# An encoder layer on one core: where the halo tokens of the first half are normalised, and where the position bias is built

## The chip, the core and the metric

The kernel runs on one core of a Trainium2 chip. A core has TensorE (matmuls; PE in the profile, its weight loads PEld), VectorE (DVE), ScalarE (ACT), GpSimd (POOL) and SyncE (SP), which issues most of the transfers between the chip's main memory and the on-chip memory SBUF. Matmuls write to the accumulator memory PSUM, of eight banks here in two groups of four. Each engine works through its own queue in order and waits on semaphores for the others. The metric is device time in microseconds (us) of one execution.

## What is computed

One residual layer for 1024 tokens of width 1024, in float32. Its matmuls run in a reduced-precision form of float32 on operands that are split in a high and a low part, so that a product is three matmuls: high x high, high x low, low x high.

```python
h = rmsnorm(x, norm1_g) * (1.0 + sc1) + sh1        # sc1, sh1: silu(c) @ w_ada + b_ada
z = h @ w_in
u, v, q, k, va, gate_a, gate_b = jnp.split(z, cuts, axis=-1)
a_out = gmlp_branch(u, v, gm_v_g, gm_w_s, gm_b_s) @ w_a
b_out = window_attention_branch(q, k, va, q_norm_g, k_norm_g, attn_sink) @ w_b
merged = jax.nn.sigmoid(gate_a) * a_out + jax.nn.sigmoid(gate_b) * b_out
x = x + gt1 * (merged @ w_o)
h2 = rmsnorm(x, norm2_g) * (1.0 + sc2) + sh2
f_gate, f_up = jnp.split(h2 @ w_ffn_in, 2, axis=-1)
x = x + gt2 * ((jax.nn.silu(f_gate) * f_up) @ w_ffn_out)
```

`rmsnorm` divides each token by the root of the mean of its squares. The attention sees 128 tokens to either side; its logits get a bias of minus slope times distance, and tokens further than 128 are masked with a very large negative number. The slope of head h (from 0) is 2 to the power of -(h+1).

## The kernel before

x is kept transposed: the 1024 features lie in eight slices of 128 partitions, tokens along the columns. The tokens are done in two halves of 512 (`half(hf)`). Since the window reaches 128 tokens over the edge, the first half needs k and v of 128 tokens of the second one as well; these are the **halo** (`xh`, eight slices of 128x128 in the tile `halo`).

The start of the first half, up to line 742: SP loads x, the condition and the first weights. While these are on the way VectorE builds the bias of four heads (`bias_base`, `build_bias`): |key - query| in `d0`, the mask in `d1`, and for each head `d0 * -slope + d1` in bfloat16. Then come squares of x, their sums over the features by matmuls with ones into `total`, and the reciprocal roots in `rcol[0]`.

The first stage is the loop over eight slices `k` (line 749; the text calls one pass of it step k). For each, VectorE scales x by the column of `mod` and by the roots (`mid<-mid,mod,ss` in the profile), ScalarE adds the shift and rounds to the high part (`h<-mid,mod`, array `hH`), VectorE makes the low part (`hL`). The columns of `mod` for the next slice are made in `ada_dot`: VectorE multiplies a slice of the modulation weights with the condition and sums, ScalarE casts a weight if there is one to cast (`cast`), and then adds the bias into `mod`. TensorE multiplies the four token tiles with 512 columns of the q weight into four banks of PSUM (`qps`), a "q pass", and with 256 columns of the k and v weight (`kps`), a "k pass", three of each per step. From step 1 on a pass of high x high comes first; the k passes of step 4 are put off to step 5 (`late`).

A q weight serves two steps, a k weight (`w_kv`) four. They are loaded whole (`raw`), then ScalarE casts the high part (`wh`) and VectorE subtracts for the low part (`wl`); `wpool` has three buffers for each of the three. Casts stand at steps 1, 3 and 5 for the next q weight and at step 4 for the second k weight. A buffer is free when the last instruction that uses it is done.

The halo in the kernel before: `load` of `xh` on SP in step 1, squares by ScalarE in step 2 into `qh`, their sums by eight matmuls with ones in step 2 between passes (`tot4[:, 0:1]`; the profile shows each as two), root and reciprocal in step 3, spread over the partitions by a transpose on TensorE in step 3. `halo_four` scales four slices (VectorE), modulates them (four ScalarE instructions) and casts; `halo_low` makes the low parts; `halo_products` multiplies with the k weight, twelve matmuls for four slices. They run for slices 0 to 3 in step 4 and for slices 4 to 7 in step 7. The other four heads of the bias are built by VectorE in step 7.

Within the loop and behind it, `in_order[0]` is set: an engine's instructions keep the order in which the program gives them. An instruction that waits therefore holds all that follow on its engine.

Behind the loop: `wvs` takes the first weight of v (`unit`: load, ScalarE cast, VectorE low part; not bound to the order), ScalarE and VectorE copy q and k out of PSUM (`qraw`, `kraw`), `v_product(k)` multiplies slice k with the v weight, `kv_norms` and `q_norm` make norms (`kms` is the profile's name for the sums of squares of k), `turn_k` transposes k on TensorE. The second half, the attention, the gates and the feed-forward part follow; the change doesn't touch them.

Of the kernel before, what the change touches and what calls it, by code (L numbers as in the profile page):

```python
# [11 lines left out]
AF = mybir.ActivationFunctionType  # L12
# [14 lines left out]
NH = 8  # L27
# [10 lines left out]
ZEROS = (9, 1)  # L38
BIAS = 4

# [66 lines left out]
def kernel(  # L107
    ctx: ExitStack,
    tc: tile.TileContext,
    xA: bass.AP,  # L110
    xB: bass.AP,
    cols: bass.AP,
    rowv: bass.AP,
# [231 lines left out]
    def bias_base():  # L345
        d0, d1 = tmp()[:, :384], tmp()[:, :384]
        G.iota(d0, pattern=[[1, 384]], base=-P, channel_multiplier=-1,
               allow_small_or_imprecise_dtypes=True)
        V.tensor_scalar(d1, d0, -1.0, None, op0=ALU.mult)
        V.tensor_tensor(d0, d0, d1, op=ALU.max)  # L350
        V.tensor_scalar(d1, d0, float(P), NEG, op0=ALU.is_gt, op1=ALU.mult)
        return d0, d1

    def build_bias(d0, d1, heads):
        for h in heads:
            V.scalar_tensor_tensor(
                out=bias[:, h, :], in0=d0, scalar=-(2.0 ** -(h + 1)), in1=d1, op0=ALU.mult,
                op1=ALU.add,
            )

# [286 lines left out]
    def half(hf):  # L647
# [4 lines left out]
        if hf == 0:  # L652
# [3 lines left out]
            halo = midt(F32, 16)  # L656
            xh, qh = halo[:, :KT, :], halo[:, KT:, :]
            hl4 = midt(F32R, 16)
# [18 lines left out]
            A.activation(sm(QPK, "es"), ones[:, :QPK], AF.Silu)  # L677
            build_bias(*base_bias, range(BIAS))

# [69 lines left out]
        for k in range(KT):  # L749
            if hf == 0:  # L750
# [25 lines left out]
                if k == 0:  # L776
                    rb = ss_tile()[:, :HALF]
                    A.copy(rb, rp)
                    kbk.append(at_bank())
                    kps = [kbk[t // 2][:, (t % 2) * 256 : (t % 2 + 1) * 256] for t in range(nkv)]  # L780
                elif k == 2:
                    A.activation(qh, xh, AF.Square)
                elif k == 3:
                    A.activation(root[:, NT:], tot4[:, 0:1], AF.Sqrt, scale=1.0 / D, bias=epsc)

# [17 lines left out]
                fours = slice(0, 4), slice(4, 8)  # L803
                if k == KT // 2:
                    halo_four(fours[0])
                    wk_halo = wk
                elif k == KT - 1:
                    halo_four(fours[1])

# [4 lines left out]
                if k == 1:  # L814
                    load(wk0[:, 512:], wk_half[1])
                    load(xh.rearrange("p a b -> p (a b)"), xA[:, KT * HALF :])
                cast = (w_next[0], raw) if src is not None else None
                if k < KT - 1:
                    ada_dot(r[:, 0, :], SC1 + k + 1, cast, dot=None if k else dot1[:, :1])
                if k == 3:  # L820
                    V.reciprocal(rcol[0][:, NT:], root[:, NT:])
                V.scalar_tensor_tensor(out=hL[k // 4][:, k % 4, :], in0=x, scalar=sh,
# [6 lines left out]
                if k < KT - 1:  # L829
                    ada_dot(r[:, 1, :], SH1 + k + 1)  # L830
                if k == KT - 1:
                    build_bias(*base_bias, range(BIAS, NH))
                if k in (KT // 2, KT - 1):
                    halo_low(fours[k == KT - 1])
                if src is not None:
# [33 lines left out]
            for group in ((q_parts, k_parts) if hf == 1 and k == 4 else (q_parts + k_parts,)):  # L869
# [14 lines left out]
                for p, (e, part) in enumerate(passes):  # L884
                    if (hf, k, p) == (0, 2, 1):
                        for a in range(KT):
                            T.matmul(tot4[:, 0:1], qh[:, a, :], ones[:, 0:1], start=a == 0, stop=a == KT - 1)
                    elif (hf, k, p) == (0, 3, len(passes) - 1):
                        T.transpose(tot4[:, P : 2 * P], rcol[0][:, NT:].to_broadcast([P, P]), ident)
                    for ps, st, w, o, n, first, last in part:  # L890
                        for e1 in ((0, 1) if e is None else (e,)):
                            T.matmul(ps, st[e1 // 2], w[e1 % 2][:, o : o + n],
                                     start=k + e1 == 0 and first,
                                     stop=bool(k == KT - 1 and e1 == 2 and last))
            if hf == 0 and k == KT // 2:
                halo_products(fours[0], wk_halo)
            if hf == 0 and k == KT - 1:
                halo_products(fours[1], wk)
            if k % 2 == 1 and k < KT - 1:
# [15 lines left out]
        kraw, banks = [], []  # L915
        for b in range(3):
            w = 512 if hf == 0 and b < 2 else 256
            r = attp.tile([P, 512], F32, tag="pt", name=nm("kraw"), bufs=6)
            (V.tensor_copy if b % 2 else A.copy)(r[:, :w], kbk[b][:, :w])
            banks.append((r, w))  # L920
            kraw += [r[:, i : i + 256] for i in range(0, w, 256)]

# [75 lines left out]
        vps = [mm_bank() for _ in range(NT)]  # L998
        wvs.append(unit(w_v[1], V))
        kr = kv_norms(banks, nkv)  # L1000
        v_product(0)
        qr = [q_norm(qraw[:, t, :]) for t in range(2)]
# [1332 lines left out]
def _layout(inputs):  # L2335
# [30 lines left out]
    for w in (w_q, w_kv):  # L2366
# [3 lines left out]
                              for t in (slice(0, 512), slice(512, 640))], axis=1),  # L2370
        "xB": xt[:, 512:],
        "cols": np.concatenate([col(a["b_ada"][0]), col(a["norm1_g"][0]), col(a["norm2_g"][0]),
                                a["gm_b_s"][0].T, col(a["c"][0])], axis=1),
# [38 lines left out]
```

## Time and profile before

| | |
|---|---|
| three runs | 1212.48, 1213.0, 1214.31 us; median 1213.0 |
| the profiled execution | 1212.33 us, its span 1210.3 us |
| granted TensorE clock | 1.0 |
| moved from and to main memory | 241.00 MB, mean 199 GB/s |
| chain that ended last | TensorE 97%, VectorE 2% of the span |

The span is the time from the first to the last instruction of the profiled execution; 2.03 us lie around it. In the profile's lists `out<-in` names the tile that is written and those that are read, with buffer numbers left out: `mm` and `at` are the two groups of PSUM banks, `mid` a pool of eight large buffers in which x, the halo, the modulation weights and others lie. Most of the lines carry L143, the helper through which engines are called, so instructions are told apart by their tiles. Matmuls overlap in their ends; how long a row of them takes is read from the starts.

### The profile page before, as it was taken

The numbers are of one execution on the slowest core, as the hardware profiler recorded it, in microseconds if no ns is written. First come the engines' busy times: TensorE is split into PE (matmuls) and PEld (weight loads), VectorE is DVE, ScalarE is ACT, GpSimd is POOL, SyncE is SP. The second block draws the span as 40 slices with busy tenths as digits, with TensorE's granted clock in tenths as the row PEclk, the third lists the DMA queues.
The fourth block names the chain that finished last, engine by engine and source line by source line (L and its number), as shares of the span: only waits on it lengthen the run. The fifth ranks groups of instructions, "written<-read, shape, count | busy, mean of one in ns | idle before, by whom it ended". The sixth has DMA issues, their size and how long they took to land.

```text
span 1210.3 us, 15628 instructions
## 1 busy us (share of the span) xinstructions
PE 1204.0 (99%) x5640; PEld 1005.0 (83%) x5640; DVE 928.4 (77%) x1503; ACT 585.8 (48%) x958; POOL 156.6 (13%) x190
## 2 busy tenths in 40 slices
PE   9999999999999999999999999999999999999998
PEld 7888888888888888888888888888888888888887
DVE  9999977889978886898987757676676765765647
ACT  6667855367855533745553333333333334433341
POOL 0124323024322000002000000010000000000001
PEclk9999999999999999999999999999999999999999
DMA  9752168753177643567313545554555449995552
GB/s 373 283 188 91 36 227 314 294 218 130 71 265 273 210 145 102 170 228 270 105 61 109 187 178 206 191 192 158 195 198 197 157 164 374 393 355 191 191 174 105
DMA packets 79709, 241.00 MB, mean 199 GB/s; under 512 B 9104, under 2 KB 9360, under 8 KB 74384
## 3 DMA queue, kind: packets, MB, share of 16 engines
q1 hardware_dynamic: 64000, 165.55, 39.1%
q0 software_dynamic: 15632, 74.46, 16.3%
q8 instruction: 44, 0.72, 0.2%
q14 instruction: 33, 0.27, 0.1%
HBM read 178.63 MB, written 61.34 MB: 198 GB/s over the span
## 4 chain that ended last, share of the span: by engine, by line
PE 97%; DVE 2%; ACT 0%; DMA 0%; issue 0%; SPq 0%; DVEq 0%; ACTq 0%
PE mm L143 49%; PE at L143 48%; DVE mid L143 1%; DVE wl L143 0%; DMA mid<-in_xA_dram 0%; ACT mid L143 0%; DVE h L143 0%; ACT wh L143 0%; ACT h L143 0%; SPq L200 0%; DVE wh L143 0%; ACT mod L143 0%; ACT cc L143 0%; DVEq L143 0%; DVE rcol L143 0%
## 5 line engine op out<-in xcount | busy, mean ns | idle before, releaser
L143 ACT CAST wh<-raw 128x1024 fp32r<-128x1024 f32 (+1 forms) x154 | 157.3, 1023 | 110.8 <-PE mm L143 45.2
L143 DVE TENSOR_TENSOR wl<-raw,wh 128x1024 fp32r<-128x1024 f32 (+1 forms) x141 | 165.3, 1176 | 53.3 <-ACT wh L143 52.7
L143 PE MATMUL mm<-mid,wh 128*128 128x512 f32 x640 | 197.4, 390 | 0.0
L143 PEld LDWEIGHTS mm<-mid,wh 128*128 128x128 f32 x640 | 119.8, 188 | 24.7
L143 PE MATMUL mm<-wh,h 128*128 128x512 f32 x384 | 124.6, 396 | 0.4 <-ACT h L143 0.3
L143 PE MATMUL mm<-mid,wl 128*128 128x512 f32 x320 | 124.5, 389 | 0.0
L143 PE MATMUL mm<-h,wh 128*128 128x512 f32 x304 | 94.3, 391 | 0.0
L143 PE MATMUL at<-h,wh 128*128 128x512 f32 x304 | 93.8, 390 | 0.0
L143 PEld LDWEIGHTS mm<-wh,h 128*128 128x128 f32 x384 | 70.8, 188 | 14.1 <-ACT h L143 0.7
L143 DVE TENSOR_TENSOR wl<-ws,wh 128x1024 fp32r<-128x1024 f32 (+1 forms) x50 | 55.9, 1117 | 24.1 <-ACT wh L143 24.1
L143 PE MATMUL mm<-wl,h 128*128 128x512 f32 x192 | 71.2, 391 | 0.0
L143 PEld LDWEIGHTS mm<-mid,wl 128*128 128x128 f32 x320 | 60.1, 188 | 12.5
L143 PEld LDWEIGHTS at<-h,wh 128*128 128x128 f32 x304 | 56.9, 188 | 11.8
L143 ACT CAST wh<-ws 128x1024 fp32r<-128x1024 f32 (+1 forms) x50 | 48.4, 968 | 37.4 <-DVE ws L143 25.0
L143 PEld LDWEIGHTS mm<-h,wh 128*128 128x128 f32 x304 | 56.6, 188 | 11.6
L143 ACT ACTIVATE t<-t 128x512 f32<-128x512 f32 x46 | 28.5, 631 | 70.8 <-DVE t L143 70.8
L143 DVE TENSOR_TENSOR ol<-raw,oh 128x1024 fp32r<-128x1024 f32 x30 | 36.6, 1224 | 30.8 <-ACT oh L143 29.1
L143 PE MATMUL mm<-h,wl 128*128 128x512 f32 x152 | 59.2, 389 | 0.0
L143 PE MATMUL at<-h,wl 128*128 128x512 f32 x152 | 59.2, 389 | 0.0
L143 ACT ACTIVATE xs<-xs 128x512 f32<-128x512 f32 x21 | 13.3, 634 | 93.7 <-DVE xs L143 93.7
L143 ACT CAST oh<-raw 128x1024 fp32r<-128x1024 f32 x30 | 31.7, 1056 | 44.1 <-PE at L143 20.0
L143 PE MATMUL at<-wl,wh 128*128 128x512 f32 (+1 forms) x136 | 52.7, 388 | 0.0
(299 smaller groups left out, 2879.7 us busy)
## 6 DMA issues: line engine op xcount, KB each, us to landing
mid<-in_w_ada_dram SPq DMA_DIRECT2D x30, 512.0 KB, 7.9
raw<-in_w_gate_dram SPq DMA_DIRECT2D x26, 512.0 KB, 4.0
tA<-hid POOLq DMA_DIRECT2D x11, 1024.0 KB, 5.2
tB<-hid POOLq DMA_DIRECT2D x11, 1024.0 KB, 5.3
wo<-in_w_out_dram POOLq DMA_DIRECT2D x22, 512.0 KB, 6.1
wS<-wo POOLq DMA_DIRECT2D x11, 1024.0 KB, 5.4
raw<-wS SPq DMA_DIRECT2D x44, 256.0 KB, 3.2
raw<-tB SPq DMA_DIRECT2D x44, 256.0 KB, 5.3
```

The costliest lines, as they stand in the source:

```text
L143: ins = f(*args, **kw)
```

## The change

The input gets one more array, `xT`: the rows of x from token 512 on, one token per partition. The rest is in `half` and the two bias functions.

- Bias: the mask becomes part of the distance, which is 1e33 larger beyond 128; a head is then a multiplication by -slope. All eight heads are built at the start, two by ScalarE and six by VectorE.
- The halo's loads (128 token rows, and `xh`) are issued in step 6. Its mean squares are made in step 6 by ScalarE from the token rows, with a sum along each row, then root, reciprocal (VectorE) and the transpose on TensorE ahead of that step's last pass.
- The first four slices of the halo are scaled and cast in step 7 and multiplied behind step 7's passes; the other four are scaled in step 7, their low parts made behind the second v weight's, their products behind `v_product(0)`. The copy of the halo's k and v out of PSUM follows those.

```diff
-        V.tensor_scalar(d1, d0, float(P), NEG, op0=ALU.is_gt, op1=ALU.mult)
-        return d0, d1
-    def build_bias(d0, d1, heads):
-        for h in heads:
-            V.scalar_tensor_tensor(
-                out=bias[:, h, :], in0=d0, scalar=-(2.0 ** -(h + 1)), in1=d1, op0=ALU.mult,
-                op1=ALU.add,
-            )
+        V.tensor_scalar(d1, d0, float(P), FAR, op0=ALU.is_gt, op1=ALU.mult)
+        V.tensor_tensor(d0, d0, d1, op=ALU.add)
+        return d0
+    def build_bias(dist):
+        for h in range(NH):
+            slope = -(2.0 ** -(h + 1))
+            if h < BIAS:
+                A.mul(bias[:, h, :], dist, slope)
+            else:
+                V.tensor_scalar(bias[:, h, :], dist, slope, None, op0=ALU.mult)
...
-            build_bias(*base_bias, range(BIAS))
+            build_bias(base_bias)
...
-                elif k == 2:
-                    A.activation(qh, xh, AF.Square)
-                elif k == 3:
-                    A.activation(root[:, NT:], tot4[:, 0:1], AF.Sqrt, scale=1.0 / D, bias=epsc)
...
                 if k == KT // 2:
+                    wk_halo = wk
+                elif k == KT - 2:
+                    load(rows_h, xT[:P, :])
+                    load(xh.rearrange("p a b -> p (a b)"), xA[:, KT * HALF :])
+                elif k == KT - 1:
                     halo_four(fours[0])
-                    wk_halo = wk
-                elif k == KT - 1:
-                    halo_four(fours[1])
...
                 if k == 1:
                     load(wk0[:, 512:], wk_half[1])
-                    load(xh.rearrange("p a b -> p (a b)"), xA[:, KT * HALF :])
...
-                if k == 3:
-                    V.reciprocal(rcol[0][:, NT:], root[:, NT:])
...
-                if k == KT - 1:
-                    build_bias(*base_bias, range(BIAS, NH))
-                if k in (KT // 2, KT - 1):
-                    halo_low(fours[k == KT - 1])
+                if k == KT - 2:
+                    A.activation(rows_h, rows_h, AF.Square, accum_out=root[:, NT:])
+                    A.activation(root[:, NT:], root[:, NT:], AF.Sqrt, scale=1.0 / D, bias=epsc)
+                    V.reciprocal(rcol[0][:, NT:], root[:, NT:])
+                elif k == KT - 1:
+                    halo_low(fours[0])
+                    halo_four(fours[1])
...
-                    if (hf, k, p) == (0, 2, 1):
-                        for a in range(KT):
-                            T.matmul(tot4[:, 0:1], qh[:, a, :], ones[:, 0:1], start=a == 0, stop=a == KT - 1)
-                    elif (hf, k, p) == (0, 3, len(passes) - 1):
+                    if (hf, k, p) == (0, KT - 2, len(passes) - 1):
                         T.transpose(tot4[:, P : 2 * P], rcol[0][:, NT:].to_broadcast([P, P]), ident)
...
-            if hf == 0 and k == KT // 2:
+            if hf == 0 and k == KT - 1:
                 halo_products(fours[0], wk_halo)
-            if hf == 0 and k == KT - 1:
-                halo_products(fours[1], wk)
...
-        for b in range(3):
+        def copy_k(b):
...
+        for b in range(2 + hf):
+            copy_k(b)
...
         wvs.append(unit(w_v[1], V))
+        if hf == 0:
+            halo_low(fours[1])
+        v_product(0)
+        if hf == 0:
+            halo_products(fours[1], wk)
+            copy_k(2)
         kr = kv_norms(banks, nkv)
-        v_product(0)
```

## What was predicted, and from what

> **What bounds the kernel now.** I read the page's list of engines first, then busy time by stretches, then the first 80 us of the timeline.
>
> ```profile
> PE 1204.0 (99%) x5640; PEld 1005.0 (83%) x5640; DVE 928.4 (77%) x1503; ACT 585.8 (48%) x958; POOL 156.6 (13%) x190
> ```
>
> ```profile
> 15.00:25.00 10.00, 9.96 (x58) 8.69 (x58) 10.00 (x16) 6.60 (x12) 0.00 (x0) 1.00 1.03 411
> ...
> 75.00:1210.30 1135.30, 1131.65 (x5229) 942.89 (x5227) 859.22 (x1361) 540.17 (x865) 145.52 (x177) 1.00 0.54 193
> ```
>
> The columns of a stretch are length, busy PE, weight load, DVE, ACT, POOL, granted clock, DMA share, GB/s. TensorE bounds the whole: after 75 us it is unbusy for 3.65 us in 1135, so a delay it carries past 75 us stays. The change lies before that, and there VectorE is as full as TensorE (10.00 of 10 from 15 to 25 us). What I need are the lengths of TensorE's and VectorE's steps; the timeline's columns are start, length, engine, operation, and idle time before.
>
> ```profile
> 23.08 0.64 PE L143 MATMUL at<-wh,h 128*128 128x256 f32 x4
> ...
> 23.26 1.04 ACT L143 ACTIVATE mid<-mid 128x1024 f32<-128x1024 f32 x1
> ...
> 23.56 1.09 PE L143 MATMUL mm<-wh,h 128*128 128x512 f32 x4
> ...
> 24.49 1.84 PE L143 MATMUL at<-ones,mid 128*128 128x1 f32 x16
> ...
> 26.20 0.72 PE L143 MATMUL at<-wh,h 128*128 128x256 f32 x4
> ...
> 27.98 0.73 ACT L143 ACTIVATE h<-mid,mod 128x512 fp32r<-128x512 f32 x1 [0.43 <-DVE mid L143]
> ...
> 28.61 0.24 ACT L143 ACTIVATE ms<-at,epsc 128x1 f32<-128x1 f32 x1
> ...
> 28.95 0.16 DVE L143 RECIPROCAL rcol<-ms 128x1 f32<-128x1 f32 x1
> ...
> 29.56 1.09 PE L143 MATMUL mm<-wh,h 128*128 128x512 f32 x4
> ...
> 32.67 0.69 DVE L143 TENSOR_TENSOR mid<-mid,at 128x512 f32<-128x512 f32 x1
> ```
>
> A q pass (four 512-wide matmuls) lasts 0.93 (23.56 to 24.49), a k pass (four 256-wide) 0.48 (23.08 to 23.56), so a step k of three of each 4.2 us. Step 2 of `half` opens at 23.56, step 3 at 29.56. The halo's sums by TensorE, between two passes, take 24.49 to 26.20, 1.71 us.
>
> ```profile
> 36.23 0.69 DVE L143 TENSOR_TENSOR mid<-mid,mid 128x512 fp32r<-128x512 f32 x1
> ...
> 36.98 0.75 DVE L143 SCALAR_TENSOR_TENSOR mid<-mid,mod,ss 128x512 f32<-128x512 f32 x1
> ...
> 37.83 0.72 ACT L143 ACTIVATE h<-mid,mod 128x512 fp32r<-128x512 f32 x1 [0.69 <-DVE mid L143]
> ...
> 38.46 1.05 ACT L143 CAST wh<-raw 128x1024 fp32r<-128x1024 f32 x1
> ...
> 38.61 1.19 PE L143 MATMUL mm<-wh,h 128*128 128x512 f32 x4 [0.19 <-ACT h L143]
> ...
> 41.74 0.75 DVE L143 SCALAR_TENSOR_TENSOR mid<-mid,mod,ss 128x512 f32<-128x512 f32 x1
> ...
> 44.35 1.09 PE L143 MATMUL mm<-wh,h 128*128 128x512 f32 x4
> ...
> 46.49 0.74 DVE L143 SCALAR_TENSOR_TENSOR mid<-mid,mod,ss 128x512 f32<-128x512 f32 x1
> 46.61 0.30 ACT L143 ACTIVATE mod<-acc_mod,cc 128x1 f32<-128x1 f32 x1 [1.42 <-DVE mid L143]
> ...
> 48.56 1.09 PE L143 MATMUL mm<-wh,h 128*128 128x512 f32 x4
> ```
>
> Steps 5, 6, 7 open on TensorE at 38.61, 44.35, 48.56. Each hangs on a chain: VectorE scales x (`mid<-mid,mod,ss`), ScalarE starts on `h` 0.85 us after that began (36.98, 37.83), and TensorE 0.06 after `h` ended. At step 5 TensorE already waits on it. VectorE runs without a gap; 41.74 to 46.49 is one of its steps, 4.75 us against 4.2 on TensorE. So in steps 3 to 7 VectorE sets the pace, and work taken from TensorE alone comes back only in part.
>
> **Start: bias.** The trace has one head by VectorE's two-operand form; the new forms are bounded by neighbours.
>
> ```profile
> 2.77 0.36 DVE L143 TENSOR_SCALAR t<-t 128x384 f32<-128x384 f32 x1
> 3.16 1.96 DVE L143 SCALAR_TENSOR_TENSOR bias<-t,t 128x384 bf16<-128x384 f32 x4
> ...
> 4.58 1.15 ACT L143 ACTIVATE mid<-mid 128x512 f32<-128x512 f32 x2 [2.35 <-DMA mid<-in_xA_dram]
> 5.76 0.69 DVE L143 TENSOR_TENSOR mid<-mid 128x512 f32<-128x512 f32 x1 [0.64 <-ACT mid L143]
> 5.89 0.63 ACT L143 ACTIVATE mid<-mid 128x512 f32<-128x512 f32 x1 [0.16 <-DMA mid<-in_xA_dram]
> ```
>
> VectorE now does a TENSOR_TENSOR (the 0.69 at 5.76 has 512 columns; I take 0.6 for 384) and six TENSOR_SCALARs: 6 x 0.39 = 2.3 (2.77 to 3.16 start to start; at most 0.49, a quarter of 1.96). From 3.16 it ends at 6.1, 0.3 past where the first add starts (5.76). ScalarE does two heads from 3.8; by its 0.63 for 512 columns, under 0.6 each, so up to 5.0, 0.4 over the first square's 4.58. But its third square waits for DMA at 5.89 anyway, and the next add waits for ScalarE. I take +0.1, bounds 0 and +0.4. The half of the bias gone from step 7 saves 1.96 of VectorE there, behind the path.
>
> **Steps 2 to 5: the gain.** Without the 1.71 TensorE is through step 2 at 24.49 + 0.48 + 0.93 + 0.48 + 0.93 + 0.48 = 27.8, but `h` of step 3 ends at 28.71: it starts at 28.8 instead of 29.56. Step 3 ends at 33.0; step 4 has three q passes and no halo products: 35.8. Step 5 then waits for VectorE, which has lost the reciprocal (0.07), the halo's scaling (0.60) and its low part (0.75, 36.23 to 36.98), in all 1.42: `h` ends at 37.13, TensorE starts at 37.2. So **-1.4** of the 1.71.
>
> **Step 5 to 6: a buffer.** `wpool` holds three weights split in two. The products of the first four halo rows need the first k weight (`wk_halo`); they move from step 4's end to step 7's. At step 5 there live that one, the q weight of steps 4 and 5, the second k weight, and the q weight of steps 6 and 7 is to be cast: a fourth.
>
> ```profile
> L143 ACT CAST wh<-raw 128x1024 fp32r<-128x1024 f32 (+1 forms) x154 | 157.3, 1023 | 110.8 <-PE mm L143 45.2
> ```
>
> Such casts do wait for matmuls elsewhere (45.2 us). Before, the cast ran at 38.46, when the halo products had just freed the buffer. Now it waits for step 5's last q pass. Step 5 runs q, three late k passes, k, q, k, q, k: from 37.2 its third q pass starts at 41.45 and ends with its last matmul at 42.5. Behind the cast on ScalarE stands `mod`, for which VectorE's scaling of step 6 waits, and so all of the chain: cast from 42.5 (1.05), `mod` (0.30) ended at 43.85, scaling 43.9, `h` from 44.75 to 45.5, TensorE at 45.5, where it was 44.35. So **+1.15**.
>
> **Step 6 to 7: the root.** The squares of token rows stand on ScalarE behind step 6's last `mod`, the reciprocal on VectorE ahead of step 7's scaling, the turn of the result on TensorE ahead of step 6's third q pass. VectorE ends step 6's dots at 43.9 + 4.75 = 48.65. Then in series: `mod` 0.12 later with 0.3 (46.61 after 46.49), square of 128x1024 1.04, the sum's read-out, root 0.24, reciprocal.
>
> ```profile
> 80.19 0.19 ACT L143 ACTIVATION_READ_ACCUMULATOR lb<-lb,nmx 128x1 f32 x1
> ```
>
> With about 0.1 overlapped at each hand-over the reciprocal runs at 50.4, scaling at 50.5, `h` from 51.35 to 52.1. TensorE waits from 48.3 for the turn, does the third passes until 52.1, and opens step 7 at 52.1: 48.56 before, so **+3.55**. Bounds of this wait of VectorE: 1.3 (square alone) to 2.1 (no overlap); I take 1.8.
>
> **End of the stage.**
>
> ```profile
> 47.96 1.64 ACT L143 ACTIVATE mid<-mid,mod 128x128 f32<-128x128 f32 x4
> ...
> 50.16 1.05 ACT L143 CAST wh<-raw 128x1024 fp32r<-128x1024 f32 x1
> ...
> 51.44 1.22 DVE L143 TENSOR_TENSOR wl<-raw,wh 128x1024 fp32r<-128x1024 f32 x1
> 51.80 1.07 ACT L143 COPY mid<-mm 128x512 f32<-128x512 f32 x2 [0.59 <-PE mm L143]
> ...
> 52.58 1.28 DVE L143 COPY mid<-mm 128x512 f32<-128x512 f32 x2
> ...
> 52.77 0.28 PE L143 MATMUL at<-wh,mid 128*128 128x256 f32 x1
> ...
> 54.21 0.40 PE L143 MATMUL mm<-wh,h 128*128 128x512 f32 x1
> ...
> 57.88 0.17 DVE L143 TENSOR_SCALAR kms<-kms 128x10 f32<-128x10 f32 x1
> ...
> 65.13 0.60 PE L143 MATMUL at<-ident,kd 128*128 128x128 f32 x4
> ```
>
> Step 7 ends at 56.3 and the first halo products (1.44, 52.77 to 54.21) at 57.75. Meanwhile ScalarE does both fours, four scalings and a cast each, 2.2 us (47.96 to 50.16); the second waits for VectorE's scaling behind the first's low part, and ends near 57.7. Only then comes the cast of w_v[0] (its buffer, too, is free only at 56), 57.7 to 58.8; before, it was over at 51.2. Then copies of q out of PSUM (0.53 each) on ScalarE to 59.8, and on VectorE low part to 60.0, copies to 61.25, k's copy to 61.9. `v_product(0)` is twelve matmuls in (65.13 - 54.21) / 4 = 2.73; its second quarter has to wait for VectorE's copy at 60.6, so it ends at 62.7. VectorE makes w_v[1]'s low part to 63.0, the halo's low part to 63.7; second halo products to 65.15. In the old trace this work is done at 54.21 + 2.73 = 56.94: **+8.2**. Last, k's norms now begin behind those products: a copy and three squares of 256 columns on ScalarE (about half of the 0.63 that 512 take at 5.89) and a reduction, so `kms` runs near 66.8. VectorE needed 65.13 - 57.88 = 7.25 from there to the turn of k, without a gap: 74.05 instead of 65.13, while TensorE would be there at 73.35. **+8.9 in all**, with 0.1 from the start 9.0.
>
> The two loads (0.5 MB each, one of them new) go out on SP behind the last modulation weights, which step 6's dots need from about 45.7. Even if those landed only then, 0.5 MB at 411 GB/s take 1.3 us, and the token rows are there at 47.0, before ScalarE squares them at 49; `xh` follows at 48.3, needed at 51. I count them at nothing; landing later, they would delay step 7 one to one. What stood behind the old load in step 1 comes 1.3 us earlier, into a VectorE that has no gap. The profiled run lasted 1212.33, its span 1210.3; 1212.33 + 9.0 = 1221.3. The median is 0.67 above that run; I forecast **1221.5**.
>
> **A page on the clock.** The new gaps of TensorE are 1.4 (35.8 to 37.2), 2.6 (42.9 to 45.5) and 2.3 us (48.3 to 50.6).
>
> ```profile
> 1.44 4.63 PE L143 MATMUL at<-zeros 128*128 128x512 f32 x10 [1.44 <-DVE zeros L143]
> ```
>
> At the start a 512-wide matmul takes 0.46, twice the later 0.23. The Trainium skill, page "TensorE: Matmul & The Clock Gate", part on the HAM clock gate, says that an idle window of about 3.4 us brings the half clock back; by it none of these gaps does so, and the sum stands. No row of this trace shows a gap that long, so the rule isn't tested here.
>
> **The rivals.**
> - *Clock lost.* Two gaps close together halve the clock for one stretch: if 3.4 us of matmuls go at 0.46 instead of 0.23, it costs some 1.7 to 3.4 us: 1224. For it: the start; against it: the granted clock of 1.00 in the stretches shown. 0.08.
> - *The buffer is free.* Were a cast not to wait for a matmul, step 6 would open at 42.9, not 45.5, and w_v[0] be limited by ScalarE alone; the other waits stay: 9.0 - 3.5 = +5.5, 1217.8. 0.12.
> - *Hidden ends.* The stalls are made good later, since VectorE and ScalarE are less full after 75 us: bounded by TensorE's 3.65 unbusy us there; only with the free buffer does it reach no change, 5.5 - 3.65 = +1.9, 1214.2. 0.08.
> - *Faster.* TensorE paces throughout: the halo's scaling and root fall beside matmuls, 1.71 is saved, and the 0.4 gap ahead of 38.61 closes: 1210.2. It decides if step 7's `h` comes before 46.8, that is, if the root's wait of 1.8 on VectorE is under 0.3 and the buffer is free. The full VectorE speaks against it. 0.07.
>
> **How the numbers follow.** The forecast, +6 to +12 about its 9.0, has 0.65. Unknown costs move it by: start -0.1 to +0.3, root's wait -0.5 to +0.3, place of w_v[0]'s cast behind the q copies +1, later absorption 0 to -3.65. The range from 1217.0 to 1225.5 takes in most of that, the freed buffer and most of the lost clock, and leaves out about 0.2. About 0.2% (2.4 us) is what a measurement tells from no change. Slower by more: 0.65 + 0.08 + 0.12 = 0.85; within: 0.08; faster: 0.07.
>
> **What would show it.** In the timeline of the changed kernel: no `at<-ones,mid` of 128x1 at 24 us; step 5 on TensorE near 37.2; a `wh<-raw` cast near 42.5 that waits for PE mm; a RECIPROCAL on VectorE near 50.4 with nearly 2 us idle before; `h` then and step 7 at 52; the second halo products near 63.7; the turn of k near 74. It would be wrong if that cast ran beside step 5 (no wait: the second rival), or if VectorE showed no gap before the reciprocal.

## The result: 0.7% slower, and the profile after

Six runs of the changed kernel gave 1221.18 to 1222.61 us, median 1221.79; six of the kernel before 1212.48 to 1214.88, median 1213.46. The ratio is 1.0068, with a 95% interval of 1.0058 to 1.0078: some 8.3 us lost. Predicted were 1221.5, between 1217.0 and 1225.5.

The profiled execution took 1221.63 us, its span 1219.8. Its page begins with busy time by engine; the second row is the chain that ended last, by engine.

```profile
PE 1205.5 (99%) x5624; PEld 1004.4 (82%) x5624; DVE 926.8 (76%) x1502; ACT 585.7 (48%) x961; POOL 156.2 (13%) x190
...
PE 94%; DVE 3%; ACT 1%; DMA 1%; issue 0%; SPq 0%; DVEq 0%; ACTq 0%
```

The sums of the halo are gone (16 matmul records fewer), and yet TensorE is busy for 1.5 us more, in a span 9.5 longer; its share of the chain fell from 97% to 94%. What TensorE waited for, from the list of waits, in us in total, times, longest:

```profile
PE mm L145 <- ACT h L145: 4.5, 3, 2.6
...
PE mm L145 <- ACT mid L145: 1.2, 1, 1.2
PE at L145 <- DVE mid L145: 1.1, 3, 0.5
...
PE at L145 <- DVE rcol L145: 0.6, 1, 0.6
PE at L145 <- DVE kd L145: 0.4, 2, 0.3
```

All five are waits in the first 75 us, which the kernel before had for 0.5 us in all (0.3 for `h`, 0.2 for `mid`). The timeline shows where they stand. The helper's line is L145 now.

```profile
43.20 1.05 ACT L145 CAST wh<-raw 128x1024 fp32r<-128x1024 f32 x1 [5.54 <-PE mm L145]
...
44.57 0.75 DVE L145 SCALAR_TENSOR_TENSOR mid<-mid,mod,ss 128x512 f32<-128x512 f32 x1 [3.64 <-ACT mod L145]
...
46.19 2.07 PE L145 MATMUL mm<-wh,h 128*128 128x512 f32 x4 [2.55 <-ACT h L145]
...
50.80 0.30 ACT L145 ACTIVATE ms<-ms,epsc 128x1 f32<-128x1 f32 x1
51.13 0.16 DVE L145 RECIPROCAL rcol<-ms 128x1 f32<-128x1 f32 x1 [1.65 <-ACT ms L145]
...
51.35 0.32 PE L145 MATMUL at<-ident,rcol 128*128 128x128 f32 x1 [0.61 <-DVE rcol L145]
...
52.91 1.09 PE L145 MATMUL mm<-wh,h 128*128 128x512 f32 x4
...
57.81 1.03 ACT L145 CAST wh<-raw 128x1024 fp32r<-128x1024 f32 x1
...
59.90 0.50 PE L145 MATMUL mm<-wh,h 128*128 128x512 f32 x1 [1.19 <-ACT mid L145]
...
63.68 0.50 PE L145 MATMUL at<-wh,mid 128*128 128x256 f32 x2 [0.49 <-DVE mid L145]
...
64.97 0.40 PE L145 MATMUL mm<-wh,h 128*128 128x512 f32 x1
...
66.87 0.17 DVE L145 TENSOR_SCALAR kms<-kms 128x10 f32<-128x10 f32 x1
...
73.50 0.30 PE L145 MATMUL at<-ident,kd 128*128 128x128 f32 x1 [0.17 <-DVE kd L145]
```

Read it from the top: the cast of the last q weight stood on ScalarE for 5.54 us and went when step 5's q pass ended; `mod`, behind it, held VectorE for 3.64 us and TensorE for 2.55. Then the root held VectorE for 1.65. Step 7 opens at 52.91, before at 48.56; the turn of k comes at 73.50, before at 65.13. That is 8.4 of the span's 9.5 (0.6 of it a later start, see below). The other 1.1 lies behind the turn, where both kernels do the same: from there to the end the profile before shows 1145.2 us, the one after 1146.3, and two others of the old order (e12 and e10 below) 1146.1 and 1147.0, so a difference of 1.1 there says nothing of the change.

In the profiles here, the first dot of VectorE (it begins when x has landed) starts between 10.58 and 11.40 us, also where the start of the kernel is the same (10.58 before, 10.93 in e12, 11.12 in e10). Where steps of two profiles are compared, that difference (0.60 between before and after) is taken out and said so.

### The profile page after: what moved, and what is told of

Read it like the earlier page. It is cut to its first block, busy times and chain, and to the rows that moved or that the text cites. A ratio compares the mean times of both kernels' runs of the same rounds, so it can differ in the third digit from the quotient of the medians.

```text
span 1219.8 us, 15598 instructions
## 1 busy us (share of the span) xinstructions
PE 1205.5 (99%) x5624; PEld 1004.4 (82%) x5624; DVE 926.8 (76%) x1502; ACT 585.7 (48%) x961; POOL 156.2 (13%) x190
## 4 chain that ended last, share of the span: by engine, by line
PE 94%; DVE 3%; ACT 1%; DMA 1%; issue 0%; SPq 0%; DVEq 0%; ACTq 0%
PE mm L145 47%; PE at L145 47%; DVE mid L145 2%; DVE wl L145 1%; DMA mid<-in_xA_dram 1%; ACT mid L145 0%; DVE h L145 0%; DVE qms L145 0%; ACT wh L145 0%; DVE vt L145 0%; DVE kd L145 0%; SPq L202 0%; DVE kms L145 0%; ACT h L145 0%; DVE kraw L145 0%
## 5 line engine op out<-in xcount | busy, mean ns | idle before, releaser
L145 ACT CAST wh<-raw 128x1024 fp32r<-128x1024 f32 (+1 forms) x154 | 157.2, 1022 | 117.9 <-PE mm L145 47.4
L145 DVE TENSOR_TENSOR wl<-raw,wh 128x1024 fp32r<-128x1024 f32 (+1 forms) x141 | 165.1, 1175 | 55.5 <-ACT wh L145 54.8
L145 PE MATMUL mm<-mid,wh 128*128 128x512 f32 x640 | 197.5, 390 | 0.0
L145 PEld LDWEIGHTS mm<-mid,wh 128*128 128x128 f32 x640 | 119.8, 188 | 24.8
L145 PE MATMUL mm<-wh,h 128*128 128x512 f32 x384 | 126.1, 400 | 5.7 <-ACT h L145 4.5
L145 PE MATMUL mm<-mid,wl 128*128 128x512 f32 x320 | 124.5, 389 | 0.0
L145 PE MATMUL mm<-h,wh 128*128 128x512 f32 x304 | 94.4, 392 | 0.0
L145 PE MATMUL at<-h,wh 128*128 128x512 f32 x304 | 93.8, 390 | 0.0
L145 PEld LDWEIGHTS mm<-wh,h 128*128 128x128 f32 x384 | 71.3, 190 | 20.3 <-ACT h L145 5.5
L145 DVE TENSOR_TENSOR wl<-ws,wh 128x1024 fp32r<-128x1024 f32 (+1 forms) x50 | 55.8, 1117 | 24.3 <-ACT wh L145 24.3
L145 PE MATMUL mm<-wl,h 128*128 128x512 f32 x192 | 71.5, 393 | 0.0
L145 PEld LDWEIGHTS mm<-mid,wl 128*128 128x128 f32 x320 | 60.1, 188 | 12.5
L145 PEld LDWEIGHTS at<-h,wh 128*128 128x128 f32 x304 | 56.9, 188 | 11.7
L145 ACT CAST wh<-ws 128x1024 fp32r<-128x1024 f32 (+1 forms) x50 | 48.3, 966 | 37.5 <-DVE ws L145 25.0
L145 PEld LDWEIGHTS mm<-h,wh 128*128 128x128 f32 x304 | 56.6, 188 | 11.6
L145 ACT ACTIVATE t<-t 128x512 f32<-128x512 f32 x46 | 28.4, 630 | 70.8 <-DVE t L145 70.8
L145 DVE TENSOR_TENSOR ol<-raw,oh 128x1024 fp32r<-128x1024 f32 x30 | 36.5, 1222 | 30.3 <-ACT oh L145 28.8
L145 PE MATMUL mm<-h,wl 128*128 128x512 f32 x152 | 59.2, 390 | 0.0
L145 PE MATMUL at<-h,wl 128*128 128x512 f32 x152 | 59.1, 389 | 0.0
L145 ACT ACTIVATE xs<-xs 128x512 f32<-128x512 f32 x21 | 13.3, 633 | 93.5 <-DVE xs L145 93.5
L145 PE MATMUL at<-wl,wh 128*128 128x512 f32 (+1 forms) x136 | 52.7, 388 | 0.0
L145 PE MATMUL at<-wh 128*128 128x512 f32 (+1 forms) x136 | 52.7, 388 | 0.0
```

Of the source, the lines that this page charges most:

```text
L145: ins = f(*args, **kw)
```

## The experiments

Theory A is the prediction's: the buffer and the root, each a wait in series on the path, then the end of the stage. Theory B is that only one of these counts, or none, because the stage has another limit just behind. A profile shows one execution of a run; where the others took another time, that is said. "Before" was run anew on the same chip with each group: 1213.80 beside the first four, 1213.23 beside the next four, then 1213.08 and 1213.55.

**e1_free: the first k weight in buffers of its own** (four of 128x512 from another pool), so that the cast finds a free buffer.

```diff
-            wq, wk = ([wpool.tile([P, UNIT], F32R, tag=x, name=nm(x)) for x in ("wh", "wl")]
-                      for _ in range(2))
+            wq = [wpool.tile([P, UNIT], F32R, tag=x, name=nm(x)) for x in ("wh", "wl")]
+            class Two:
+                def __init__(self):
+                    self.parts = [attp.tile([P, 512], F32R, tag="pt", name=nm("wk"), bufs=6)
+                                  for _ in range(2)]
...
+            wk = [Two(), Two()]
```

> Changed kernel with the first k weight's split parts kept in four 128x512 buffers of another pool that stand unused in this stage, so that casts of the q weights wait for no matmul. Theory (three waits in a row, each paid for: buffer, root, end of stage): the cast of step 5 runs beside step 5, step 6 opens on TensorE near 43.5 instead of 46.2, the wait of VectorE for the root stays, and the time is 3.5 us under the changed kernel, 1218.3. Rival (the root hides the buffer, one wait swallowing the other): step 7 opens near 52.9 as before, and the time stays within 0.7 us of the changed kernel, 1221.8.

1221.43 us, ratio 1.0064 [1.0049, 1.0079]: the wait was gone, the time was not. ScalarE's timeline around the root:

```profile
47.95 0.18 ACT L145 ACTIVATION_READ_ACCUMULATOR mid<-mid 128x1 f32 x1
48.43 1.04 ACT L145 CAST wh<-raw 128x1024 fp32r<-128x1024 f32 x1 [0.29 <-DMA raw<-in_w_v_dram]
49.38 0.29 ACT L145 ACTIVATE ms<-ms,epsc 128x1 f32<-128x1 f32 x1
```

Between the sum's read-out and the root now stands the cast of w_v[0]. It is not bound to the program's order; its buffer used to be free only at the end of step 7, and now is free at step 6. It waits for its transfer, holds the root, and its low part on VectorE holds the reciprocal: TensorE's wait for the turn grew to 3.35 us. The rival's time came true, but not for its reason: the root alone did not hold step 7, the slipped cast did. Then TensorE's clock fell, as the stretch from 50 to 60 us shows (third number from the right):

```profile
50.00:60.00 10.00, 9.14 (x40) 7.97 (x41) 5.71 (x11) 4.58 (x11) 0.92 (x1) 0.67 0.45 159
```

0.67 over 10 us is a half clock for some 6.7. The profiled execution is the slowest of the four (1222.72, the others 1220.86 to 1221.77). A freed buffer let another instruction in at a worse place.

**e2_root: the root out of the way.** Token rows loaded in step 4, squared in step 5 ahead of the cast that waits there, reciprocal in step 5.

```diff
-                elif k == KT - 2:
                     load(rows_h, xT[:P, :])
                     load(xh.rearrange("p a b -> p (a b)"), xA[:, KT * HALF :])
+                elif k == KT - 3:
+                    A.activation(rows_h, rows_h, AF.Square, accum_out=root[:, NT:])
+                    A.activation(root[:, NT:], root[:, NT:], AF.Sqrt, scale=1.0 / D, bias=epsc)
...
-                if k == KT - 2:
+                if k == KT - 3:
                     V.reciprocal(rcol[0][:, NT:], root[:, NT:])
```

> Changed kernel with the halo's loads issued in step 4 and square and root of its token rows on ScalarE in step 5 ahead of the cast that waits there, the reciprocal in step 5 too. Theory: the reciprocal no longer stops VectorE, TensorE no longer waits for the turn; the buffer's wait and the end of the stage stay. If TensorE keeps its clock in step 6, step 7 opens 1.9 us earlier than the 52.9 of the changed kernel: 1219.9. If the granted clock falls again behind the gap ahead of step 6, the slow matmuls, which the root's wait hid, come on the path: only 0.9 earlier, 1220.9. Rival (the root was never on the path, since slow matmuls fill the time anyway): no change, 1221.8.

1221.68 us (1219.68 to 1221.88), ratio 1.0065 [1.0048, 1.0082]: no gain in the median. In TensorE's timeline the first wait stands as it was, and the turn waits for nothing:

```profile
45.69 1.21 PE L145 MATMUL mm<-wh,h 128*128 128x512 f32 x4 [2.55 <-ACT h L145]
...
49.77 0.41 PE L145 MATMUL at<-ident,rcol 128*128 128x128 f32 x1
...
58.25 0.50 PE L145 MATMUL mm<-wh,h 128*128 128x512 f32 x1 [0.77 <-ACT mid L145]
```

The profiled execution took 1219.68, two less than the other three of this kernel (1221.62 to 1221.88). Their mean granted clock is 0.998, that of the profiled one 0.999, but they left no trace, so what they lost stays open; e5 tries the clock as its cause.

**e3_both: the edits of e1 and e2 together.**

> Changed kernel with both edits, free buffer and early root. Theory: what is left is the end of the stage (halo's scalings on ScalarE ahead of the casts and copies, k's norms behind the second halo products), less the 1.4 us won by step 5: 5.2 us under the changed kernel, 1216.6, so 3.2 over the kernel before; step 7 opens near 47.7. Rival (buffer and root are all there is, and without them the change wins its 1.7): 1211.8.

1215.75 us in ten runs, ratio 1.0017 [1.0008, 1.0026]. Alone the two edits bring 0.4 and 0.1 us against the changed kernel's 1221.79, together 6.0. The changed kernel was not run again beside them; reckoned from the before of each group (+8.3 for the change, +7.6, +7.9 and +2.0 here) they bring 0.7, 0.5 and 6.4. The time is 0.85 under the theory's 1216.6, far from the rival's 1211.8. With both, the root is done before w_v[0]'s cast can slip in ahead of it, and the cast of the last q weight waits for nothing. But 2.0 us over before are left. TensorE's timeline:

```profile
28.89 1.18 PE L145 MATMUL mm<-wh,h 128*128 128x512 f32 x4 [0.90 <-ACT h L145]
...
37.35 1.20 PE L145 MATMUL mm<-wh,h 128*128 128x512 f32 x4 [1.29 <-ACT h L145]
...
47.41 1.09 PE L145 MATMUL mm<-wh,h 128*128 128x512 f32 x4
...
52.28 1.45 PE L145 MATMUL at<-wk,mid 128*128 128x256 f32 x10 [0.22 <-DVE mid L145]
...
57.38 0.51 PE L145 MATMUL at<-wh,mid 128*128 128x256 f32 x2 [0.66 <-DVE mid L145]
...
58.68 0.40 PE L145 MATMUL mm<-wh,h 128*128 128x512 f32 x1
...
67.20 0.30 PE L145 MATMUL at<-ident,kd 128*128 128x128 f32 x1 [0.18 <-DVE kd L145]
```

Of 3.15 us that leave TensorE ahead of step 5 (sums 1.71, first halo products 1.44), 2.19 come back as waits for `h`. Step 7 opens at 47.41, 1.15 sooner than before (1.29 with the first dot's 0.14 taken off). Then the halo products that were put off, 1.44 with two waits of 0.22 and 0.66, come in between: `v_product(1)` starts at 58.68, before at 56.94, 1.74 later; the turn of k comes 1.93 later, with the first dot's 0.14 taken off. Before, those products had stood where TensorE would else have waited.

**e4_bias: the kernel before with the new bias alone.**

> Kernel before with only the bias part of the change: all eight heads at the start, two by ScalarE. Theory: nothing measurable, +0.1 us, 1213.6; the first sums of x start within 0.1 us of the kernel before. Rival (the start of the changed kernel, where VectorE was 0.6 us later at 11.2, comes from the bias): +0.6, 1214.1, and the fourth and later squares of x later in the trace.

1213.76 us in ten runs, ratio 0.9997 [0.9988, 1.0006]. The interval, from 1.5 us faster to 0.7 slower, shows no cost and no gain of the bias.

**e5_root_fill and e6_fill: eleven matmuls with zeros ahead of step 6**, into the accumulator of q with nothing to add, in e2_root and in the changed kernel. They keep TensorE going through the gap of 2.55 us.

```diff
+                if (hf, k) == (0, KT - 2):
+                    keep_going(qps[0], zeros, zeros, 11)
```

> The early root once more, with eleven matmuls of zeros added to a bank ahead of step 6, 2.6 us of work that fills the gap in which TensorE waits for the buffer. They add nothing to the sums. Theory (the gap lets the clock fall to half for one or two spells of 3.4 us, and in the early-root kernel TensorE is the bound there, so each costs up to 1.7): the granted clock stays at 1.00 and the time falls to about 1219.9, from 1221.7. Rival (the slow matmuls hide behind VectorE in this kernel as well): within 0.5 us of 1221.7.

> The changed kernel with the same eleven matmuls of zeros ahead of step 6 and nothing else. Theory (the root's wait ends last in step 6, and the slow matmuls were done within it): the clock stays at 1.00 from 45 to 50 us, TensorE waits about 2.2 us for the turn instead of 0.6, the time stays within 0.5 us of 1221.8. Rival (the fallen clock is one of the costs of the change): 1220.2 or below.

1221.36 us (1220.87 to 1221.45), ratio 1.0065 [1.0052, 1.0079], and 1222.04 (1221.94 to 1222.62), ratio 1.0073 [1.0059, 1.0086]. The granted clock stayed at 1.00 in both profiled executions (in e6_fill two of the four runs show a mean of 0.998 all the same, at 1221.96 and 1222.12, no slower than the others). In the changed kernel, where it had been lower (stretches; the clock is the number third from the right):

```profile
45.00:50.00 5.00, 3.81 (x12) 3.26 (x13) 4.49 (x8) 1.67 (x4) 0.00 (x0) 0.66 0.54 204
```

0.66 over 5 us is a half clock for 3.4. Without it, in TensorE's timeline of e6_fill:

```profile
50.98 0.32 PE L145 MATMUL at<-ident,rcol 128*128 128x128 f32 x1 [2.09 <-DVE rcol L145]
```

TensorE was sooner at the turn and waited there 2.09 us instead of 0.61; the turn of k comes 62.32 us after the first dot in both. So the lost clock cost the changed kernel nothing. In e5_root_fill step 5 to step 7 took 13.21 us instead of 14.45, but that came back behind step 7: the turn of k comes 61.18 us after the first dot, in e2's profile 61.17. So the one spell of half clock in e2's profile (0.72 from 45 to 50 us, 0.94 from 50 to 55) cost nothing up to there. Why its other three runs took two us more stays open; they show a lower mean clock, but without any loss of clock e5_root_fill took as long.

**e7_free_order: e1_free with the cast of w_v[0] bound to the program's order.**

```diff
         qs = [midt(F32R, 16), midt(F32R, 16)]
+        in_order[0] = hf == 0
         wvs = [unit(w_v[0], V)]
```

> The free buffer once more, with the first v weight's cast and low part bound to the program's order, so that they can't slip ahead of the root and the reciprocal as they did (cast of 1.04 and its wait for a DMA on ScalarE, low part of 1.2 on VectorE). Theory: VectorE's wait at the root is 1.8 us again, TensorE's gap ahead of the turn near 1.5 instead of 3.35, the clock doesn't fall, step 7 opens near 49.5, and the time is 1217.5. Rival (the buffer's wait costs nothing of its own, the root alone holds step 7): 1221.4 as without the order.

1219.37 us (1218.36 to 1220.73), ratio 1.0048 [1.0033, 1.0064]: 2.4 better than the changed kernel, between the two numbers. The four runs are two pairs: 1218.36 and 1218.55 with a mean clock of 1.000, 1220.19 (the profiled one) and 1220.73 with 0.999. ScalarE's timeline:

```profile
47.66 0.19 ACT L145 ACTIVATION_READ_ACCUMULATOR mid<-mid 128x1 f32 x1
47.88 0.29 ACT L145 ACTIVATE ms<-ms,epsc 128x1 f32<-128x1 f32 x1
...
55.01 0.62 ACT L145 CAST mid<-mid 128x512 fp32r<-128x512 f32 x1
55.54 1.04 ACT L145 CAST wh<-raw 128x1024 fp32r<-128x1024 f32 x1
```

Now the root follows at once. Step 5 to step 7 takes 11.47 us instead of 15.20, 3.7 less. But the cast of w_v[0], kept in order, comes behind the halo's last cast (55.01), and `v_product(0)` waits 1.35 for the copy behind it. After that wait the clock fell, as a stretch and TensorE's timeline show:

```profile
55.00:60.00 5.00, 3.36 (x14) 2.42 (x13) 3.39 (x5) 3.97 (x6) 0.00 (x0) 0.83 0.21 48
```

```profile
57.12 0.49 PE L145 MATMUL mm<-wh,h 128*128 128x512 f32 x1 [1.35 <-ACT mid L145]
...
58.23 0.95 PE L145 MATMUL mm<-wh,h 128*128 128x512 f32 x2
```

From 60 to 65 us it is 0.83 again, together a half clock for 3.4 us. Two matmuls take 0.95 (at full clock 0.62), and `v_product(0)` lasts from 57.12 to 62.10, of which 0.28 is a wait, where 2.73 is its length at full clock: 2.0 us lost, the difference of the two pairs. So with the clock kept, in two runs, the free buffer is worth 3.1 to 3.3 us (1218.5 is 5.2 over its own before and 3.3 under the changed kernel), and the theory's 1217.5 is missed by one.

**e8_rows_only: the kernel before with the mean squares from token rows alone**: rows loaded in step 1, `xh` in step 2, the halo otherwise where it was; the sums on TensorE left away.

> The kernel before with one thing of the change: the halo's mean squares by ScalarE from token rows (square in step 2, root in step 3 as before), so that TensorE's 1.71 us of sums go; loads of rows and halo in steps 1 and 2, everything else in its old place. Theory (VectorE paces up to step 5): TensorE gains in steps 2 and 3 and waits that long at steps 3 and 5; step 5 opens at 38.5 as before, and the time is 1213.4, within 0.4 us of the kernel before. Rival (TensorE paces): -1.7, 1212.0.

1214.47 us in eleven runs, ratio 1.0011 [1.0002, 1.002]: 1.2 us more than before, and no gain from the 1.71 us of sums. Neither number held. VectorE's timeline, in the slowest of these runs (1215.77), gives a reason:

```profile
30.71 1.23 DVE L144 SCALAR_TENSOR_TENSOR mid<-mid,silu_c 128x1024 f32<-128x1024 f32 x1 [1.31 <-DMA mid<-in_w_ada_dram]
```

The added 0.5 MB stood ahead of the modulation weights while the DMA share of the stretches was 1.0 and more; VectorE waited 1.31 us, and TensorE behind it.

**e9_both_pool and e10_before_pool: weights' low parts by GpSimd.** After e3_both the suspect for the 2.0 us left was VectorE's pace. Four low parts of 1.14 us each go to GpSimd, in e3_both and, as a control, in the kernel before.

```diff
-                        low_part(w, w0, slice(0, UNIT))
+                        low_part(w, w0, slice(0, UNIT), G)
```

> Kernel e3_both with one thing more: the 1024-wide low parts of the q and k weights of the first stage (steps 2, 4, 5, 6; 1.14 us each on VectorE) by GpSimd, which is idle there. Theory (with the two waits gone, what is left is VectorE's pace of 4.75 us a step against TensorE's 4.2, so that neither the 1.71 us of the sums nor the move of the halo products can pay): VectorE gets 4 x 1.14 = 4.6 us, step 7 opens some 2 us sooner than in e3_both and the time is about 1213.5, at best 1211.8. Rival (the end of the stage, where ScalarE and VectorE copy and cast for the halo and the v weights, or the transfers set the end): step 7 opens sooner, but the turn of k does not, and the time stays within 0.6 of e3_both's 1215.75.

> The kernel before, with those low parts by GpSimd and nothing of the change. It is the control of e9_both_pool. Theory: TensorE has only 0.4 us of waits in the first stage of the kernel before (0.19 ahead of step 5 and a few more), so the freed 4.6 us of VectorE bring at most 0.4: 1213.0 to 1213.6. Rival (VectorE's pace hides more, in matmuls that start late one by one without a gap that the list of waits shows): 1212.0 or below; slower than 1214 if GpSimd's 2.4 us a low part come too late for TensorE.

1221.03 us, ratio 1.0068 [1.0055, 1.008], and 1222.14, ratio 1.0072 [1.0059, 1.0086]: the control alone lost 9 us, so the test says nothing of the suspect. Neither number of e9_both_pool held; the control's last case, slower than 1214, came true, but by the delay of VectorE that follows. From the timeline of e10_before_pool:

```profile
21.74 2.44 POOL L143 TENSOR_TENSOR wl<-raw,wh 128x1024 fp32r<-128x1024 f32 x1 [20.00 <-ACT wh L143]
...
21.85 3.42 DVE L143 SCALAR_TENSOR_TENSOR mid<-mid,silu_c 128x1024 f32<-128x1024 f32 x1
...
26.81 1.56 PE L143 MATMUL mm<-wh,h 128*128 128x512 f32 x4 [1.90 <-ACT h L143]
...
32.89 3.23 POOL L143 TENSOR_TENSOR wl<-raw,wh 128x1024 fp32r<-128x1024 f32 x1 [8.70 <-ACT wh L143]
...
33.78 2.88 DVE L143 SCALAR_TENSOR_TENSOR mid<-mid,mod,ss 128x512 f32<-128x512 f32 x1
```

VectorE's dot takes 3.42 us instead of 1.22 while GpSimd subtracts, its scaling 2.88 instead of 0.75, and GpSimd in turn 3.23 instead of 2.44 where VectorE was first. Four such delays of VectorE, 2.0 to 2.2 us each, outweigh the 4.6 that it was to win. The clock was at half for 6.8 and 3.4 us as well; what part of the 9 us is its was not tried. The Trainium skill, page "SBUF — State Buffer", section "SBUF: two separate sides", says that a VectorE operation with two inputs in SBUF and a GpSimd operation that reads SBUF hold one pair of ports as an exclusive lock, and whoever comes second waits to the end. The rows agree.

**e11_both_nolow and e12_before_nolow: the same low parts left out.** TensorE multiplies with the high part in their place, as many matmuls on other data.

```diff
-                    w_next = [wpool.tile([P, UNIT], F32R, tag=x, name=nm(x)) for x in ("wh", "wl")]
+                    w_next = [wpool.tile([P, UNIT], F32R, tag=x, name=nm(x)) for x in ("wh",)] * 2
...
-                    lows.append((w_next, raw))
```

> e3_both without the 1024-wide low parts of the weights in the first stage (steps 2, 4, 5, 6): TensorE multiplies with the high part in their place, so the same matmuls run on other data, and VectorE has 4 x 1.14 = 4.6 us less work there. Theory (VectorE's pace is why taking the sums from TensorE does not pay): the waits of TensorE for ScalarE's h in the first stage (2.2 us in e3_both) go, and the time falls from 1215.75 to about 1213.5, within 0.8 of e12_before_nolow. Rival (the end of the stage, with its halo casts and copies, sets the end whatever step 7 does): 1215.0 or more, and over 1.5 above e12_before_nolow.

> The kernel before, with the same low parts left out and nothing of the change: the control of e11_both_nolow. TensorE waits for next to nothing in the first stage of the kernel before (0.19 at step 5), so both theories expect no more than 0.4 from the freed VectorE: 1213.0 to 1213.6. If it falls below 1212, VectorE held TensorE there as well, and the difference to e11_both_nolow is what counts.

1215.58 us in eleven runs, ratio 1.0019 [1.001, 1.0028], and 1213.53, ratio 1.0002 [0.9993, 1.0011]. So 4.6 us less on VectorE bring nothing in either. In the kernel before, TensorE has hardly a wait that they could shorten. The timeline of e11_both_nolow, ahead of step 5, shows why they bring nothing there:

```profile
34.31 1.05 ACT L145 CAST wh<-raw 128x1024 fp32r<-128x1024 f32 x1 [2.99 <-DMA raw<-in_w_kv_dram]
...
35.68 0.75 DVE L145 SCALAR_TENSOR_TENSOR mid<-mid,mod,ss 128x512 f32<-128x512 f32 x1 [2.20 <-ACT mod L145]
...
37.30 1.20 PE L145 MATMUL mm<-wh,h 128*128 128x512 f32 x4 [2.33 <-ACT h L145]
```

and its stretch from 25 to 35 us:

```profile
25.00:35.00 10.00, 9.97 (x54) 8.25 (x52) 8.47 (x15) 4.07 (x7) 0.00 (x0) 1.00 1.02 415
```

VectorE is no longer full (8.47 of 10), yet step 5 opens at 37.30, in e3_both at 37.35. The second k weight lands only at 34.3, with the DMA engines full (1.02) at 415 GB/s; its cast holds `mod`, this VectorE, this TensorE. It is the early loads of e2's edit that stand ahead of it: the token rows and `xh`, 1 MB, are issued at 19.93 and 21.30, the weight at 21.82 (in e3_both likewise, and its cast waits 1.90 for the transfer). In the changed kernel the loads stand behind the weight, and its cast waits for a matmul, no longer for the transfer:

```profile
23.75 0.33 SPq L202 DMA_DIRECT2D raw<-in_w_kv_dram  x1
...
25.73 0.43 SPq L202 DMA_DIRECT2D mid<-in_xT_dram  x1
...
33.36 1.05 ACT L145 CAST wh<-raw 128x1024 fp32r<-128x1024 f32 x1 [0.46 <-PE mm L145]
```

So in e3_both the transfers are a second limit at the place where VectorE was the suspect, and the early loads made it; what VectorE's pace alone is worth in the changed kernel, this pair does not tell. The rival's number held, but not its reason: step 7 opened as late as in e3_both.

## Why the prediction was right

The time was right, and the terms of its sum are in the trace. That it came within 0.3 us holds some luck: the sum of 9.0 was added to the profiled execution of 1212.33, the lowest of all times of the kernel before, the end of the stage came out 1.1 shorter, and the later start and the 1.1 behind the turn put that back. With the 0.60 of the later start taken off, as everywhere in this list:

- *Start, bias +0.1*: measured 0, by e4_bias. The 0.60 is the landing of x, which varies nearly as much without the change (0.54 in e10_before_pool).
- *Steps 2 to 5, -1.4, step 5 at 37.2*: step 5 opened at 37.71, so at 37.1. Right in size. Its reason, that VectorE paces and has lost 1.42, fits the trace of the changed kernel, where VectorE is busy without a gap from 20 to 40 us and the weight's cast does not wait for its transfer. No run tests it: in e11_both_nolow, which relieves VectorE, the transfers had become the limit.
- *Step 5 to 6, a buffer, cast at 42.5, step 6 at 45.5*: 42.6 and 45.6. e1_free and e7_free_order show that it was this buffer: with another one the wait is gone.
- *Step 6 to 7, the root, VectorE's wait 1.8, step 7 at 52.1, +3.55*: 1.65, and step 7 at 52.3, +3.75. TensorE's own wait for the turn was 0.61, not 2.3, because its matmuls ran at the half clock before it; at full clock, in e6_fill, it was 2.09.
- *End of the stage, w_v[0]'s cast 57.7, `v_product(0)` to 62.7, second halo products to 65.15, kms 66.8, turn 74.05*: 57.2, 62.2, 64.4, 66.3, 72.9. It came out 1.1 better: 0.5 because the unbound cast went ahead of the halo's second cast, not behind it, and 0.6 because from kms to the turn it took 6.63 (66.87 to 73.50), not the 7.25 of before. The later start put 0.6 of it back.

What failed is not in the sum but beside it. First, the page on the clock: step 6 stood behind a gap of 2.55 us (predicted 2.6), and the clock was at half for 3.4 us. The Trainium skill's rule of an idle window of about 3.4 us ("TensorE: Matmul & The Clock Gate", Part 1, "What's actually happening") would have kept it up, and the prediction went by it; here the measurement decides. e6_fill shows that this cost nothing here, since the root held TensorE at the turn anyway. So in the changed kernel the rival "clock lost" had its event, but not its price of 1.7 to 3.4; in e7_free_order, where no other wait took it up, such a spell cost 2.0.

Second, the price of the rival "the buffer is free" (-3.5): in e1_free 0.4, in e7_free_order 2.4. The wait itself was priced about right, as the 3.1 to 3.3 of e7's two runs at full clock show. What the price left out is what the edit sets off besides: in e1_free an unbound cast moved ahead of the root, and the gaps that were left cost clock. So the waits can't simply be taken off one by one: the two edits alone bring 0.4 and 0.1, together 6.0.

Of the other rivals, "hidden ends" did not come: behind the turn of k nothing was made good. "Faster" hung on a step 7 whose `h` comes before 46.8; it came at 52, since the buffer wasn't free and VectorE waited 1.65 for the root.

Where the time went, then: some 6.4 of the 8.3 us are the two waits together (the change costs 8.3 over its before, e3_both 2.0 over its own). The other 2.0, as the timeline of e3_both reads, are the halo's first products, moved from a place where TensorE waits anyway to one where it does not, with the waits of the new end; no run moved them back alone. Of the 3.15 us taken from TensorE ahead of step 5, e3_both still has 1.3 when step 7 opens; of the 1.71 of sums alone, e8_rows_only has none. But in both, as in e11_both_nolow, moved loads had put a transfer in the way; what the sums would bring with transfers to spare was not tried. No version here is measurably faster than the kernel before.

## What to carry to other kernels

When work is moved later, ask which buffers its operands hold on to, and which instruction, queued in order, waits for one of them: it was one weight kept for three steps more that stopped three engines. Here matmuls taken out of a stage where VectorE and the transfers are as full as TensorE came back as waits, and work that had filled such waits was paid in full where it was moved to. Two waits in one stage are tested together as well as singly, since taking one away moves what stands behind it. And an experiment that moves a load is checked for what that load now stands ahead of; its runs are compared at equal clock.

## What the runs showed of the hardware

- The granted clock fell after gaps of TensorE shorter than 3.4 us, and the length of the gap alone doesn't decide: behind 1.35 us (e7_free_order, 0.28 more soon after) and 2.55 us (the changed kernel) stood a half clock for 3.4 us, behind 1.90 us (e10_before_pool) and 3.35 us (e1_free) one of 6.8 us each; behind 2.09 us (e6_fill) and 2.33 us (e11_both_nolow) none.
- VectorE and GpSimd did not work side by side where each had two inputs in SBUF: 0.75 us became 2.88, 1.22 became 3.42.
- A transfer of 0.5 MB put ahead of others went with a wait of 1.31 us on VectorE at a DMA share of 1.0 (e8_rows_only); 0.5 MB at 415 GB/s are 1.26.
